# RWKV final states of the samples: made inside the chunk chain, their two products tied behind the entry's, and the spread tokens on VectorE instead of GpSimd

## The chip, the cores and the metric

One core of one Trainium2 chip runs the whole program in one launch. The metric is the device time of that core in microseconds (us); three runs of the kernel before gave 986.63, 986.88 and 988.02, median 986.88. A core has engines that each work through a queue of their own in order: TensorE (PE, with its weight loads PEld), VectorE (DVE), ScalarE (ACT), GpSimd (POOL) and SyncE (SP), which only issues DMAs here. They wait for each other through semaphores.

## The reference

One layer of a hybrid decoder: RWKV-7 time mixing and differential attention side by side, gates, an MLP, for 512 prompt tokens and 8 samples of 8 tokens each. The change touches RWKV's state for the samples:

```python
def step(S, inp):
    r_t, w_t, k_t, v_t, a_t, b_t = inp
    sa = jnp.einsum('bhij,bhj->bhi', S, a_t)
    S = S * w_t[:, :, None, :] + sa[..., None] * b_t[:, :, None, :] + v_t[..., None] * k_t[:, :, None, :]
    return S, jnp.einsum('bhij,bhj->bhi', S, r_t)

S, ys = lax.scan(step, S0.astype(jnp.float32), xs)
```

There are 8 heads of width 64, and the state `S` of each of the 8 samples after its 8 tokens is an output (`rwkv_sample`, here `Ss`), as is the prompt's (`Sp`).

## The kernel before

The scan is done in chunks of 64 tokens. Chunks 0 to 7 are the prompt; chunk 8 holds the 64 sample tokens, sample by sample. Heads go in pairs: head pair `hp` (0 to 3) fills 128 partitions, `par` 0 and 1 are its two heads. Two head pairs (`e` 0 and 1) share a chain: `chain(0)` runs pairs 0 and 1, `chain(1)` pairs 2 and 3.

`rwkv(hp)` is a generator in stages, parted by `yield`; `run(...)` takes the next stage of each pair that it names. The first stage makes decays, keys and the masked products `pA` (tiles `pn`, `pw`, `pa`, `pbn`, `KB`, `ST`, `pA`, `ABR`); then come the turned values `SVU`, the turned keys `KBt`, and the inverse `TT`. The stage that the change cuts is the one after `TT` (from L943): it spreads the solved tokens of chunk 8 over the samples, `vm = SVU[:, 8, par]` times a mask (128x512, one for each `par`), multiplies with `KBt` (product `pF`, two matmuls, each with 64 columns of weights and so into one half of `pF`'s partitions), adds the entering state `s0`, scales by the decay `pc`, and stores `Ss`.

A step of the chain for chunk `ci` (L1044 on): the entry (16 passes, `pch<-SVU,ST`), the copy `R` on VectorE, the solve (`pch<-R,TT`), the leaves of the chunk before (`pch<-SVU,ABR`), the copy of the solved `SVU` by VectorE and ScalarE together, the product with `KBt`, the new state `S<-S,pc,pch`, and `SVU<-S,pc` on both engines for the next entry. Chunk 8 is solved beside chunk 1, so its `SVU` is there from chunk 2 on.

TensorE's time between these steps is filled with dense products (`ps_z`, `ps_g`, `ps_brb`: 288 columns of tokens each). They stand in `waiting`; `take(n)` issues n of them at a low priority, and a scheduler that sorts each engine's instructions by priority, once their inputs are there by its own estimate, lays the final order. `tc.issue_after(x)` ties an instruction to a place behind `x`. `bank` gives one of three PSUM buffers (tag `w`), `tile(tag="G", bufs=3)` one of three SBUF buffers, which `vm` shares with other tiles; `s0` has two.

## Time and profile before

| | |
|---|---|
| median of three runs | 986.88 us |
| the profiled execution | 984.4 us, span 982.6 us |
| granted TensorE clock | 0.996 |
| chain 0 | about 284 to 327 us |
| chain 1 | about 432 to 475 us |
| `pF` products | 288.6 to 294.0 us and 482.8 to 486.9 us |
| `vm` on GpSimd, 8 of them | 1033 to 1043 ns each, 287.5 to 485.8 us |

The page gives busy time and share of the span by engine. The timeline gives start, length, engine, line, operation, tiles and count of instructions; what stands in brackets is the idle time of that engine ahead of it, and what ended it. A matmul's length covers its way through the array, so matmuls overlap: what one costs is read from the starts. An f32 matmul is recorded as two passes.

### The profile page before, as it was taken

The page shows a single profiled execution, that of the slowest core. Times are in us where ns is not written, and L with a number is a line of the kernel's source. Part 1 is how long each engine was busy: PE and PEld are TensorE (multiplying, and loading weights), DVE is VectorE, ACT ScalarE, POOL GpSimd, SP SyncE. Part 2 cuts the span into 40 slices and gives each one's busy share as a digit, 9 for nine tenths or more (in the row PEclk, how much of TensorE's full clock was granted, in tenths as well). Part 3 has the DMA queues.
Part 4 walks back from the last instruction along what each step waited for, and adds up shares of the span by engine and source line. Part 5 has one row for each costly group of instructions (what it writes and reads, how often), then busy time and mean ns, then how long its engine had stood idle before and what let it go on. Part 6 is the DMA issues. An engine that isn't in the chain of part 4 may idle for free.

```text
span 982.6 us, 24623 instructions
## 1 busy us (share of the span) xinstructions
PE 951.1 (97%) x10120; PEld 898.2 (91%) x10120; DVE 676.1 (69%) x1427; ACT 507.2 (52%) x1120; POOL 72.8 (7%) x181
## 2 busy tenths in 40 slices
PE   8999999999999998999999999999999999999996
PEld 8999989887978997878899999999999999999996
DVE  6698566875556848354787989966666666666744
ACT  6576455565345464543354767444444444444732
POOL 2611100100010210001300000000000000000001
PEclk9999999999999999999999999999999999999998
DMA  7422663201212225221477532222222232220402
GB/s 267 141 71 72 207 222 118 86 26 45 67 57 77 94 88 190 70 83 58 173 239 234 179 121 86 87 86 87 86 87 87 90 93 93 92 86 23 140 1 97
DMA packets 50833, 105.75 MB, mean 108 GB/s; under 512 B 6066, under 2 KB 8114, under 8 KB 50594
## 3 DMA queue, kind: packets, MB, share of 16 engines
q1 hardware_dynamic: 47442, 96.95, 30.6%
q0 software_dynamic: 1648, 5.35, 1.6%
q10 hardware_dynamic: 1632, 1.89, 0.6%
q8 instruction: 79, 1.29, 0.5%
q14 instruction: 32, 0.26, 0.1%
HBM read 89.38 MB, written 14.78 MB: 106 GB/s over the span
## 4 chain that ended last, share of the span: by engine, by line
PE 56%; DVE 2%; ACT 1%; DMA 1%; issue 1%; POOL 0%; DVEq 0%
PE ps_dn L72 20%; PE ua L1261 5%; PE ux L1261 5%; PE ps_wo L72 4%; PE ps_g L72 4%; PE ps_brb L72 3%; PE ps_bra L72 3%; PE uc L1261 3%; PE ub L1261 3%; PE ud L1261 2%; PE pch L1021 2%; DMA raw_dn<-in_w_down_dram 1%; PE pW L72 1%; PE pZ L72 0%; DVE ya L61 0%
## 5 line engine op out<-in xcount | busy, mean ns | idle before, releaser
L72 PE MATMUL ps_dn<-q,hi_dn 128*128 128x288 f32 x768 | 154.7, 296 | 0.0
L72 PEld LDWEIGHTS ps_dn<-q,hi_dn 128*128 128x128 f32 x768 | 122.8, 188 | 1.5
L72 PE MATMUL ps_dn<-q,lo_dn 128*128 128x288 f32 x384 | 113.2, 295 | 0.0
L72 PE MATMUL ps_g<-xh,hi_g 128*128 128x288 f32 x256 | 77.7, 303 | 1.0 <-DVE gg L61 1.0
L72 PE MATMUL ps_g<-xh,lo_g 128*128 128x288 f32 x256 | 78.5, 307 | 0.0
L72 PE MATMUL ps_g<-xl,hi_g 128*128 128x288 f32 x256 | 78.2, 305 | 0.0
L72 PEld LDWEIGHTS ps_dn<-q,lo_dn 128*128 128x128 f32 x384 | 72.0, 188 | 0.0
L72 PE MATMUL ps_z<-xh,lo_z 128*128 128x288 f32 (+1 forms) x224 | 69.7, 311 | 0.0
L72 PE MATMUL ps_z<-xl,hi_z 128*128 128x288 f32 (+1 forms) x224 | 67.2, 300 | 0.0
L72 PE MATMUL ps_z<-xh,hi_z 128*128 128x288 f32 (+1 forms) x224 | 67.1, 299 | 0.0
L61 DVE TENSOR_TENSOR ya<-ya,ps_dn 128x288 f32<-128x288 f32 x96 | 43.3, 451 | 27.6 <-PE ps_dn L72 27.5
L58 ACT ACTIVATE hi_dn<-raw_dn 128x512 fp32r<-128x512 f32 x48 | 30.1, 628 | 56.2 <-PE ps_dn L72 56.1
L58 ACT ACTIVATE c<-c 128x288 f32<-128x288 f32 x112 | 48.7, 439 | 9.4 <-DVE c L61 7.7
L1261 PE MATMUL ux<-h_t,hi 128*128 128x288 f32 x256 | 52.4, 297 | 0.0
L1261 PE MATMUL ua<-h_b,hi 128*128 128x288 f32 x256 | 52.2, 296 | 0.0
L72 PEld LDWEIGHTS ps_g<-xh,hi_g 128*128 128x128 f32 x256 | 48.2, 188 | 2.5 <-issue 1.4
L72 PEld LDWEIGHTS ps_g<-xl,hi_g 128*128 128x128 f32 x256 | 48.2, 188 | 1.8 <-issue 0.5
L58 ACT ACTIVATE hi<-a 128x1024 fp32r<-128x1024 f32 (+1 forms) x32 | 27.1, 846 | 43.3 <-PE ps_dn L72 34.9
L72 PEld LDWEIGHTS ps_g<-xh,lo_g 128*128 128x128 f32 x256 | 48.1, 188 | 1.4
L72 PE MATMUL ps_dn<-q,w 128*128 128x320 f32 (+1 forms) x336 | 46.6, 298 | 0.8 <-DVE fin L61 0.8
L72 PEld LDWEIGHTS ps_dn<-q,w 128*128 128x128 f32 x336 | 45.3, 190 | 1.2 <-DVE fin L61 1.1
L61 DVE TENSOR_TENSOR lo<-s,hi 128x1024 fp32r<-128x1024 f32 x32 | 39.2, 1224 | 10.4 <-ACT hi L58 10.3
(390 smaller groups left out, 2730.6 us busy)
## 6 DMA issues: line engine op xcount, KB each, us to landing
a<-in_w_up_dram SPq DMA_DIRECT2D x32, 512.0 KB, 3.3
raw_dn<-in_w_down_dram SPq DMA_DIRECT2D x64, 256.0 KB, 2.8
raw_g<-in_w_in_dram SPq DMA_DIRECT2D x32, 256.0 KB, 3.1
raw_z<-in_w_in_dram SPq DMA_DIRECT2D x28, 256.0 KB, 2.9
gt_d<-gg SPq DMA_DIRECT2D x16, 288.0 KB, 2.8
g<-gt_d SPq DMA_DIRECT2D x16, 288.0 KB, 3.7
kp<-in_ktab_dram SPq DMA_DIRECT2D x16, 256.0 KB, 3.5
vp<-in_vtab_dram SPq DMA_DIRECT2D x16, 256.0 KB, 3.5
```

What stands on the lines that cost most here:

```text
L58: ring["act"] = AE.activation(out=out, in_=in_, func=func, **kw)
L61: ins = (eng or VE).tensor_tensor(out=out, in0=a, in1=b, op=op)
L72: ring["mm"] = PE.matmul(out=out, lhsT=lhsT, rhs=rhs, start=start, stop=stop)
L1021: ring["mm"] = PE.matmul(out=ps[rows, e], lhsT=lhs, rhs=rhs, start=first and e == 1, stop=True, skip_group_check=True)
L1261: ring["mm"] = PE.matmul(out=ps[:, :288], lhsT=l[:, k], rhs=hb[blk][:, h, k], start=start and i == 0, stop=i == 11, skip_group_check=skip)
```

## The change

The stage after `TT` is cut in two by a new `yield`: first the two `vm`, now on VectorE (`GE` is gone from the call), then the two products and the rest. The two products are tied, the first behind the last matmul issued before, the second behind the first. `chain` now runs these two stages itself, right after the entry of a chunk: in chunk 2 the first pair's `vm`, in chunk 4 the first pair's products and the second pair's `vm`, in chunk 6 the second pair's products. So the matmul that the first product is tied to is the entry's last. The calls of `run` around the chains lose the stages that the chains took over.

```diff
@@ -940,15 +940,19 @@
         own[e] = ST, KBt, TT, ABR, pc
         yield
 
-        pF = bank(f"pF{hp}")
         vms = []
         for par in range(2):
             vm = rt.tile([P, NB, 64], F32, tag="G", bufs=3, name=f"vm{hp}{par}")
             tt(vm, m3(SVU[:, 8, par], NB),
-               c[:, C_MB:C_MB + NB].rearrange("p (b o) -> p b o", o=1).broadcast_to([P, NB, 64]), MUL, GE)
+               c[:, C_MB:C_MB + NB].rearrange("p (b o) -> p b o", o=1).broadcast_to([P, NB, 64]), MUL)
             vms.append(vm)
+        yield
+
+        pF = bank(f"pF{hp}")
+        lead = ring["mm"]
         for par, rows in halves:
-            mm(pF[rows], KBt[:, 8, par], vms[par].rearrange("p b i -> p (b i)"))
+            with tc.issue_after(lead.ins):
+                lead = mm(pF[rows], KBt[:, 8, par], vms[par].rearrange("p b i -> p (b i)"))
         sn = s0
         tt(sn, s0, pF.rearrange("p (b i) -> p b i", b=NB), ADD)
@@ -1041,9 +1045,12 @@
         owed = []
+        states = {2: (0,), 4: (0, 1), 6: (1,)}
         for ci in range(8):
             here = [(cbank(ci % 2, f"pch{pr}{ci}"), ci)]
             R = entry(*here[0])
+            for hp in states.get(ci, ()):
+                next(gens[2 * pr + hp])
             if ci == 1:
@@ -1098,7 +1105,7 @@
     chain(0)
-    run(0, 1, 2)
+    run(2)
     take(310)
@@ -1109,7 +1116,7 @@
     chain(1)
     take(226)
-    run(2, 3, 2, 3)
+    run(2, 3)
```

Where this moves instructions, first TensorE in chain 0. Before, the first product `pF0` stands ahead of the entry of chunk 2; behind that entry follow (`pch02<-R02` is the solve, `ABR` the leaves, `pn2` the beginning of head pair 2's first stage):

```order
L72 MATMUL pF0_4768<-vm01_4771,KBt0_2885 64x512
L72 MATMUL pF1_4778<-vm10_4779,KBt1_3722 64x512
L1021 MATMUL pch02_4558<-R02_4567,TT1_4432 64x64 x2
L1021 MATMUL pch02_4558<-R02_4567,TT0_3527 64x64 x2
L1021 MATMUL pch01_4508<-SVU0_2871,ABR1_3657 64x64 x2
L1021 MATMUL pch01_4508<-SVU0_2871,ABR0_2819 64x64 x2
L1021 MATMUL pch08_4519<-SVU0_2871,ABR1_3657 64x64 x2
L1021 MATMUL pch08_4519<-SVU0_2871,ABR0_2819 64x64 x2
L72 MATMUL pF1_4778<-vm11_4781,KBt1_3722 64x512
L72 MATMUL pn2_4790<-cst_sb_75,sq_2_4788 128x2 x5
```

Now the two `pF0` stand between entry and solve of chunk 4, the two `pF1` between those of chunk 6:

```order
L1025 MATMUL pch06_4709<-SVU0_2871,ST0_0_2814 64x64
L72 MATMUL pF1_4720<-vm10_4650,KBt1_3722 64x512
L72 MATMUL pF1_4720<-vm11_4652,KBt1_3722 64x512
L1025 MATMUL pch06_4709<-R06_4718,TT1_4432 64x64 x2
L1025 MATMUL pch06_4709<-R06_4718,TT0_3527 64x64 x2
L1025 MATMUL pch05_4676<-SVU0_2871,ABR1_3657 64x64 x2
L1025 MATMUL pch05_4676<-SVU0_2871,ABR0_2819 64x64 x2
L72 MATMUL pn2_4790<-cst_sb_75,sq_2_4788 128x2 x5
L72 MATMUL pw20_4818<-P12_1817,wl_215 128x288
L72 MATMUL pa20_4821<-P12_1817,al_216 128x288
L1025 MATMUL pch06_4709<-SVU0_2871,KBt1_3722 64x64 x2
```

So the products of one head pair stand together, and head pair 2's first stage begins in chunk 6 instead of chunk 2. Before, its products `pA2` stood at the end of chain 0, among chunk 7's product with `KBt` and its leaves; now 83 matmuls of fill lie between `pn2` and `pA2`, and `pA2` comes after the chain.

VectorE in chain 0 around chunk 2 (`SVU0<-pch01` and `<-pch08` are the solved chunks 1 and 8, `S01` the state after chunk 1, `R02` the copy behind the entry of chunk 2). Before:

```order
L1036 COPY SVU0_2871<-pch08_4519 64x2x64
L66 SCALAR_TENSOR_TENSOR S01_4551<-S00_4502,pc0_2791,pch01_4508 128x64
L66 SCALAR_TENSOR_TENSOR S01_4551<-S00_4502,pc1_3629,pch01_4508 128x64
L69 TENSOR_SCALAR SVU0_2871<-S01_4551,pc0_2791 64x64
L69 TENSOR_SCALAR SVU0_2871<-S01_4551,pc1_3629 64x64
L1029 COPY R02_4567<-pch02_4558 128x128
L61 TENSOR_TENSOR s0_0_2907<-s0_0_2907,pF0_4768 128x512
```

Now:

```order
L1040 COPY SVU0_2871<-pch08_4519 64x2x64
L61 TENSOR_TENSOR vm00_4569<-SVU0_2871,cst_sb_75 128x512
L66 SCALAR_TENSOR_TENSOR S01_4551<-S00_4502,pc0_2791,pch01_4508 128x64
L66 SCALAR_TENSOR_TENSOR S01_4551<-S00_4502,pc1_3629,pch01_4508 128x64
L69 TENSOR_SCALAR SVU0_2871<-S01_4551,pc0_2791 64x64
L69 TENSOR_SCALAR SVU0_2871<-S01_4551,pc1_3629 64x64
L61 TENSOR_TENSOR vm01_4571<-SVU0_2871,cst_sb_75 128x512
L61 TENSOR_TENSOR vm10_4650<-SVU0_2871,cst_sb_75 128x512
L1033 COPY R02_4567<-pch02_4558 128x128
```

Three of the four `vm` stand around that step; the fourth, `vm11`, comes behind `R04`, followed by the addition `s0<-s0,pF0` and then the copy `SVU0<-pch04`.

TensorE in chain 1. Before, the four products stand far behind the chain, among the dense products `ps_brb`:

```order
L72 MATMUL ps_brb_3_0_7427<-obh4_7094,lo_brb_3_0_7424 128x288
L72 MATMUL pF2_7438<-vm20_7439,KBt2_5393 64x512
L72 MATMUL pF2_7438<-vm21_7441,KBt2_5393 64x512
L72 MATMUL pF3_7448<-vm30_7449,KBt3_6226 64x512
L72 MATMUL pF3_7448<-vm31_7451,KBt3_6226 64x512
L72 MATMUL ps_brb_3_0_7427<-obh6_7100,hi_brb_3_0_7423 128x288
```

Now, in chunk 4 (and with `pF3` in chunk 6):

```order
L1025 MATMUL pch14_6945<-SVU2_5371,ST0_2_4866 64x64
L72 MATMUL pF2_6956<-vm20_6881,KBt2_5393 64x512
L72 MATMUL pF2_6956<-vm21_6883,KBt2_5393 64x512
L1025 MATMUL pch14_6945<-R14_6954,TT3_6696 64x64 x2
L1025 MATMUL pch14_6945<-R14_6954,TT2_6137 64x64 x2
L1025 MATMUL pch13_6912<-SVU2_5371,ABR3_5533 64x64 x2
```

The fills that stood between entry and solve of those chunks stand behind the leaves now, and the entries of chunks 5 and 6, which had fill between their first matmul and the other seven, stand whole. On GpSimd, `vm31` stood behind two powers `var`; none of the eight `vm` is left there. In SP's queue the loads of `s0` for pairs 2 and 3 stand two and four weight loads later.

## The prediction

> **What bounds the kernel now.** I read the page first, then the waits, then the timeline around the two stretches that hold the products `pF`.

> ```profile
> span 982.6 us, 24623 instructions
> PE 951.1 (97%) x10120; PEld 898.2 (91%) x10120; DVE 676.1 (69%) x1427; ACT 507.2 (52%) x1120; POOL 72.8 (7%) x181
> ```

> The reader is to see that TensorE (PE) is busy 97% of the span, VectorE (DVE) only 69%, ScalarE 52% and GpSimd (POOL) 7%. The dense work ("fill": the `ps_` matmuls) is put between the steps of the chain, so a microsecond counts only if PE stands still in it, or if PE does the same work in fewer slots. PE idles 982.6 - 951.1 = 31.5 us in all: no removal of waits can bring more than that. The same number of matmuls is issued after the change, so I look for idle time at `pF`, for products that run beside each other, and for changes between fill and chain matmuls.

> Chain 0, the timeline of PE (start, length, engine, line, tile):

> ```profile
> 288.63 1.07 PE L72 MATMUL pF<-vm,KBt 128*64 128x512 f32 x2
> 289.27 0.33 PE L1021 MATMUL pch<-SVU,ST 128*64 128x64 f32 x2
> 290.69 0.62 PE L1021 MATMUL pch<-SVU,ST 128*64 128x64 f32 x13 [0.98 <-DVE SVU L69]
> ...
> 291.20 1.02 PE L72 MATMUL pF<-vm,KBt 128*64 128x512 f32 x3
> 292.16 0.45 PE L1021 MATMUL pch<-R,TT 64*64 64x64 f32 x8
> ...
> 293.00 1.07 PE L72 MATMUL pF<-vm,KBt 128*64 128x512 f32 x2
> 294.00 1.28 PE L72 MATMUL pn<-cst_sb,sq 128*128 128x2 f32 x10
> ```

> One f32 product is two passes, so `x2` is one product. In chain 0 the first and the last of the four run alone for about 1 us each; only the middle two share the array. Within them the entry of chunk 2 stops after two passes and PE waits 0.98 us for VectorE's `SVU<-S`. The next view says why that is late:

> ```profile
> 287.54 4.05 POOL L61 TENSOR_TENSOR vm<-SVU,cst_sb 128x512 f32<-128x512 f32 x4 [30.84 <-DMA gt_d<-gg]
> ...
> 288.71 1.92 DVE L69 TENSOR_SCALAR SVU<-S,pc 64x64 f32<-64x64 f32 x2
> ...
> 319.47 0.40 DVE L69 TENSOR_SCALAR SVU<-S,pc 64x64 f32<-64x64 f32 x2
> ...
> 442.00 3.05 POOL L61 TENSOR_TENSOR vm<-SVU,cst_sb 128x512 f32<-128x512 f32 x3 [4.18 <-DVE SVU L1036]
> 442.65 1.44 DVE L69 TENSOR_SCALAR SVU<-S,pc 64x64 f32<-64x64 f32 x2
> 444.15 0.68 PE L1021 MATMUL pch<-SVU,ST 128*64 128x64 f32 x14 [0.50 <-DVE SVU L69]
> ```

> The same two `SVU<-S` instructions take 0.40 us where GpSimd is quiet, and 1.92 and 1.44 us while it makes `vm`. They end at 290.63 and 444.09; whole `vm` instructions of about 1.02 us end near 290.6 (the third) and 444.05 (the second). So VectorE is held until a `vm` is done. In both chains PE then waits, 0.98 and 0.50 us.

> The products of chain 1 come much later, behind the chain:

> ```profile
> 482.58 0.29 PE L72 MATMUL ps_brb<-obh,lo_brb 128*128 128x288 f32 x1
> 482.81 1.93 PE L72 MATMUL pF<-vm,KBt 128*64 128x512 f32 x6
> 485.87 1.07 PE L72 MATMUL pF<-vm,KBt 128*64 128x512 f32 x2 [1.13 <-POOL vm L61]
> 486.87 0.54 PE L72 MATMUL ps_brb<-obh,hi_brb 128*128 128x288 f32 x2
> ```

> The fourth `vm` is late (in GpSimd's order two powers of `var` stand ahead of it), and PE waits 1.13 us for it. Three products in 1.93 us, and one alone in 1.0 (485.87 to 486.87): a pair that is ready takes about 0.95 us, hardly more than one.

> **The change part by part.** The four edits have one answer on PE, so I work them out by stretch. First the price of an edge between fill and chain work, which each regrouping pays:

> ```profile
> 463.99 0.29 PE L72 MATMUL ps_g<-xh,lo_g 128*128 128x288 f32 x1
> 464.21 0.33 PE L1021 MATMUL pch<-SVU,ST 128*64 128x64 f32 x2
> 464.47 0.40 PE L72 MATMUL ps_g<-xh,hi_g 128*128 128x288 f32 x1
> 464.70 0.30 PE L72 MATMUL ps_g<-xl,hi_g 128*128 128x288 f32 x1
> 464.84 0.29 PE L72 MATMUL ps_g<-xh,lo_g 128*128 128x288 f32 x1
> 465.06 0.68 PE L1021 MATMUL pch<-SVU,ST 128*64 128x64 f32 x14
> 465.67 0.40 PE L72 MATMUL ps_g<-xh,hi_g 128*128 128x288 f32 x1
> 465.91 0.30 PE L72 MATMUL ps_g<-xl,hi_g 128*128 128x288 f32 x1
> ```

> This is one entry of 16 passes, cut in two by three fills. Fill follows fill in 0.13 to 0.14 us (464.70 to 464.84). Going in costs 465.06 - 464.84 - 0.13 = 0.09, coming out 465.91 - 465.67 - 0.13 = 0.11: 0.2 us per group of chain matmuls. The 14 passes alone cost 1.07 - 2 x 0.13 = 0.81, so a whole entry, two passes of 0.04 more, about 0.85. The cut one costs 463.99 to 465.91 less its five fill slots, 1.92 - 0.66 = 1.26: a cut is 0.4 us dearer.

> Chain 0, removed: from 288.63 less the edge (288.54) to 294.00 are 5.5 us. There remain the entry (0.85) and the solve with two leaves (292.16 to 293.00, 0.84, and one pair of edges, 0.2): 1.89. So **-3.6 us**, with the 0.98 of waiting in it.

> Added: two pairs, each tied right behind an entry in chunks 4 and 6 and followed by the solve. I take 1.05 us a pair, between 1.0 for one alone and 1.07 for the middle two with their run-out (the row of 291.20 is their second half; the solve begins at 292.16). The fills that stood between entry and solve go elsewhere, which saves one pair of edges, 0.2: 2 x 0.85 = **+1.7 us**.

> Moved: the last products of chain 0 and the first stage of the third head pair (`pn2` to `pA2`) no longer share groups; by the order of PE two groups more at the end: **+0.4 us**.

> Chain 1: the stretch 482.71 to 486.87 goes, with its edges 4.2 us (1.13 waiting in it); two pairs come, +1.7; the wait of 0.50 at 444.15 goes; and two entries that were cut in two (chunks 5 and 6) stand whole: 2 x 0.4 = 0.8. Sum -4.2 + 1.7 - 0.5 - 0.8 = **-3.8 us**.

> On VectorE: eight `vm`. No row shows one there; the nearest on the same engine is

> ```profile
> L61 DVE TENSOR_TENSOR s<-a 128x512 f32<-128x512 f32 x16 | 10.9, 684 | 0.0
> ```

> and above it lies GpSimd's own pace (3.05 us for three). I take 0.68, same shape and engine: 5.5 us of VectorE in all, 8.1 at the upper end. On the path it costs 0 if all lie in gaps and 5.5 (8.1) if none does; a gain below zero is left out, as the waits that GpSimd caused are counted above. I take 0 because of where they stand: `vm00` falls before `S<-S` of chunk 1, in VectorE's gap after the copies of chunk 1; `vm01` and `vm10` lie under nine and seven fills (1.2 and 0.9 us). The tightest are `vm11` and `vm31`, which must wait for a first product to give its buffer back, with the addition `s<-s,pF` behind them and then the chain's own copy `SVU<-pch`. For that the latency of a plain step, from solve to copy:

> ```profile
> 317.12 0.45 PE L1021 MATMUL pch<-R,TT 64*64 64x64 f32 x8
> ...
> 317.62 0.28 DVE L1036 COPY SVU<-pch 64x128 f32<-64x128 f32 x1 [0.82 <-PE pch L1021]
> ```

> From the start of an entry: products done at about 1.6, `vm11` to 2.25, addition to 2.9, copy to 3.2, ScalarE's half of it, as long again, to 3.5 us. PE reaches the product with `KBt` after pair, solve, leave and eleven fills at 0.5 + 1.0 + 0.3 + 0.3 + 1.65 = 3.75. The margin is 0.2 us: free, but barely. Without that cover each of the two places costs what it is late.

> The stage `pn2` to `pA2` gets shorter. Its rows on PE, and the window over it (PE, PEld, DVE, ACT, POOL busy, then clock and DMA):

> ```profile
> 297.03 0.65 PE L72 MATMUL pw<-P,wl 128*128 128x288 f32 x2
> ...
> 325.22 0.43 PE L72 MATMUL pA<-ST,KB 64*64 64x128 f32 x2
> 294.00:326.00 32.00, 31.59 (x349) 26.24 (x348) 21.01 (x55) 17.01 (x42) 2.88 (x12) 1.00 0.26 86
> ```

> It was spread over 294.00 to 325.22, 31.2 us, with VectorE busy two thirds of the window (21.01 of 32). In the new order 83 fills (11.0 us), six groups of chain work (0.5 to 0.85 each, some 3.5) and the stage's own matmuls (`pn` 1.28, six like the `pw` above, whose 0.65 overlaps with the next, at 0.5) stand between: about 18.5 us. Of VectorE's 21 us some 16 fall into it, since three of the five chain steps of that window now run earlier (four operations of 0.28 to 0.47 us each, 1.6 a step). It fits, but closely, and PE would wait at `pbn` or `pA`. Bounds: 0, and 31.2 - 18.5 = 12.7 if it takes as long as before; I take **+0.5**, near the lower, because there VectorE followed the chain and was not full.

> SP's two loads of `s0` move behind weight loads, which are issued ahead of their use, so I cost it at nothing. GpSimd's stores of the states come earlier, or a few microseconds later; nobody waits.

> Sum: -3.6 + 1.7 + 0.4 - 3.8 + 0.5 = **-4.8 us**. The profiled execution took 984.4 us (span 982.6), so 979.6; the median of the runs shown is 986.88, 2.5 above it, and gives **982.1 us**.

> **Rivals.** (a) VectorE becomes what the chain waits for: no gap takes a `vm`, each delays a step by some 0.62 us that fill does not hide. Then 8 x 0.62 = 5.0 comes back: 987.1, no change. For it: margins of 0.2. Against it: VectorE idles a third of that stretch. [...]

> (b) The slower one: the shortened stage. VectorE's and ScalarE's work from `pn2` to `pA2` lasts longer than the 18.5 us of PE work laid over it, and PE, in order, waits at `pbn2` and `pA2`. It has eaten the gain when PE waits 5.3 us there, makes the kernel measurably slower from 7.3 us, and at the full 12.7 gives 982.1 - 0.5 + 12.7 = 994.3. For it: the 16 us of VectorE in 18.5. Against it: in the window VectorE stood idle a third of the time, waiting for the chain.

> (c) The change does not do what it says on one point: `SVU<-S` was not held by GpSimd but by its place in the chain. Then 0.98 + 0.50 stays: 983.6. Against it: both ends fall on the end of a `vm`.

> (d) The tied pairs don't run beside each other: four times 0.95 more, 985.9. Against it: six passes in 1.93 us.

> **How the numbers follow.** Forecast 0.60 (its own range 980 to 984), (a) 0.14, (b) 0.08, (c) 0.08, (d) 0.06, others 0.04. A measurement of this kernel can tell about 0.2%, 2 us, from no change. Faster by more than that: the forecast, (c) and part of the rest, 0.74; within: (a), (d) and some of (b), 0.18; slower 0.08. The range leaves out the lower half of the forecast's tail and most of (b) and reaches to (d) and nearly to (a): 979.3 to 986.6.

> **What would show it.** Right: no wait above 0.3 us at an entry for `SVU L69`; `SVU<-S` pairs at 0.40 us everywhere; four passes of a `pF` pair within 1.1 us, four times; no `pF` behind 480 us; no `vm` on POOL. Wrong: waits on PE at `pbn` or `pA` for VectorE over 1 us (b); waits at `KBt` products of chunk 4 for `SVU` (a); a pair in 2 us (d); a `SVU<-S` pair still over 1 us (c). A PE idle sum that falls by less than 2 us makes the prediction wrong.

## The result and the profile after

The changed kernel takes 977.75 us (median of 4 runs, 977.14 to 980.07) beside 986.75 before (median of 4): ratio 0.9915, interval 0.9892 to 0.9939. Run once more without an edit, beside 29 runs of before, it took 977.24 against 985.12: 0.9923, interval 0.9909 to 0.9938. The prediction said 982.1, with a range of 979.3 to 986.6: the direction was right, and the forecast gain of 4.8 us was about half of the 9.0 between these medians. The page of the changed kernel begins:

```profile
span 978.3 us, 24613 instructions
PE 948.2 (97%) x10120; PEld 898.2 (92%) x10120; DVE 677.1 (69%) x1435; ACT 508.5 (52%) x1120; POOL 64.8 (7%) x173
```

The two profiled spans differ by 4.3 us only (982.6 and 978.3), which is less than the medians say. The page can't tell why; the same fill matmuls, read in both traces, can. First before, then after: start, length, engine, line, tile, of four fills of the same count, ahead of chain 0, behind the stage that follows it, ahead of chain 1 and behind its products.

```profile
287.29 0.40 PE L72 MATMUL ps_g<-xh,lo_g 128*128 128x288 f32 x1
...
357.38 0.38 PE L72 MATMUL ps_g<-xh,hi_g 128*128 128x288 f32 x1
...
433.68 0.30 PE L72 MATMUL ps_brb<-obh,hi_brb 128*128 128x288 f32 x1
...
492.56 0.30 PE L72 MATMUL ps_brb<-obh,lo_brb 128*128 128x288 f32 x1
```

```profile
289.18 0.40 PE L72 MATMUL ps_g<-xh,lo_g 128*128 128x288 f32 x1
...
356.17 0.38 PE L72 MATMUL ps_g<-xh,hi_g 128*128 128x288 f32 x1
...
432.47 0.29 PE L72 MATMUL ps_brb<-obh,hi_brb 128*128 128x288 f32 x1
...
487.78 0.29 PE L72 MATMUL ps_brb<-obh,lo_brb 128*128 128x288 f32 x1
```

Between the first two, and between the last two, both kernels issue the same matmuls, only in another order. The changed kernel starts the first of these fills 1.89 us later, the second 1.21 earlier, the third 1.21 earlier and the fourth 4.78 earlier. So chain 0 with what follows gained **3.1 us**, chain 1 **3.6 us**, 6.7 together, and the 1.89 was lost before any changed instruction ran. Half of it is in this row of the windows (PE, PEld, DVE, ACT, POOL busy, then the granted clock), of after and of before:

```profile
6.00:12.00 6.00, 5.58 (x28) 5.36 (x29) 4.60 (x7) 5.46 (x10) 1.60 (x4) 0.72 1.01 364
```

```profile
6.00:12.00 6.00, 5.31 (x35) 4.85 (x36) 4.71 (x7) 5.38 (x10) 1.41 (x3) 1.00 1.01 363
```

In this one execution of the changed kernel the clock of TensorE stood at 0.72 of full in that window (28 matmuls for 35); the other profile of it does not show that, and gains the same in the two stretches: 3.1 and 3.6 us. The rest of the 1.89 lies in small steps between 215 and 285 us that I did not follow up.

Chain 0 on VectorE, in answer to the rows with 1.92 us:

```profile
289.38 0.69 DVE L61 TENSOR_TENSOR vm<-SVU,cst_sb 128x512 f32<-128x512 f32 x1
...
290.60 0.40 DVE L69 TENSOR_SCALAR SVU<-S,pc 64x64 f32<-64x64 f32 x2
290.92 1.28 DVE L61 TENSOR_TENSOR vm<-SVU,cst_sb 128x512 f32<-128x512 f32 x2
```

The pair of `SVU<-S` takes 0.40 us, and one `vm` 0.69 (0.68 was taken). On PE, chunk 6 of chain 0:

```profile
314.16 0.69 PE L1025 MATMUL pch<-SVU,ST 128*64 128x64 f32 x16
314.67 1.03 PE L72 MATMUL pF<-vm,KBt 128*64 128x512 f32 x4
315.63 0.45 PE L1025 MATMUL pch<-R,TT 64*64 64x64 f32 x8
```

Entry, pair, solve: the four passes of two products take 1.03 us (1.05 was taken), and so in three of the four places. In chunk 4 of chain 0 one pass of the entry stands between the first pass and the other three, and the four span 1.13 us.

**Where the 3.1 us of chain 0 come from.** A matmul's slot is the time from its start to the start of the next. The slots of the same matmuls between the first two fills above, summed by kind:

| kind | before, us | after, us | difference |
|---|---|---|---|
| entries `pch<-SVU,ST` (96) | 5.21 | 3.70 | -1.51 |
| products `pF` (8 passes) | 2.64 | 1.97 | -0.67 |
| `pA` (72) | 3.18 | 2.48 | -0.70 |
| `pbn` (4) | 0.85 | 0.54 | -0.31 |
| fills (301), with edges | 46.71 | 46.16 | -0.55 |
| `pK` (9) | 1.25 | 1.60 | +0.34 |
| `pch<-SVU,ABR` (64) | 2.37 | 2.59 | +0.22 |
| `pw` (4) | 1.06 | 1.16 | +0.10 |

The first two lines are what the prediction counted. `pA` and `pbn` belong to the stage that it expected to lose. The line of `pK` is a wait of 0.44 us for ScalarE that before did not have. Before, the passes of `pA` were mixed with the last steps of the chain:

```profile
325.22 0.43 PE L72 MATMUL pA<-ST,KB 64*64 64x128 f32 x2
325.58 0.45 PE L1021 MATMUL pch<-SVU,KBt 128*64 128x64 f32 x8
325.96 0.65 PE L72 MATMUL pA<-ST,KB 64*64 64x128 f32 x12
326.67 0.27 PE L1021 MATMUL pch<-SVU,ABR 64*64 64x64 f32 x2
326.70 0.32 PE L72 MATMUL pA<-ST,KB 64*64 64x128 f32 x1
...
328.88 1.29 PE L72 MATMUL pA<-ST,KB 64*64 64x128 f32 x32 [0.51 <-DVE ABR L61]
```

After, they stand together, and PE waits a little longer for the mask:

```profile
335.46 1.32 PE L72 MATMUL pA<-ST,KB 64*64 64x128 f32 x40
...
338.11 1.29 PE L72 MATMUL pA<-ST,KB 64*64 64x128 f32 x32 [0.73 <-DVE ABR L61]
```

The wait rose from 0.51 to 0.73, but 72 passes in two groups cost less than in six. The line of the fills hides a wait that is gone. Before, VectorE and then PE, behind the stage:

```profile
345.47 0.76 DVE L61 TENSOR_TENSOR y<-y,var 128x576 f32<-128x576 f32 x1 [1.91 <-POOL var L243]
346.15 0.45 DVE L61 TENSOR_TENSOR gg<-ps_g,R 128x288 f32<-128x288 f32 x1
...
346.75 0.37 PE L72 MATMUL ps_g<-xh,hi_g 128*128 128x288 f32 x1 [0.99 <-DVE gg L61]
```

VectorE stood 1.91 us for GpSimd's `var` with the drain of a fill's bank (`gg`) queued behind it, and PE stood 0.99. With the later stage VectorE has other work ahead of that point, and PE does not wait.

**Where the 3.6 us of chain 1 come from.** By the same count the products `pF` give 2.14, the entries 1.52, and the fills lose 0.08. In the fills stands a new wait, ahead of the last fill that the comparison uses:

```profile
484.09 0.50 PE L72 MATMUL ps_brb<-obh,hi_brb 128*128 128x288 f32 x2 [0.69 <-DVE gb L66]
```

It is a drain once more (`gb` empties a bank of `ps_brb`): VectorE came to it late, after 1.49 us of waiting for GpSimd's `var`.

### The profile page after: what moved, and what is told of

Read it like the earlier page. It is cut to its first block, busy times and chain, and to the rows that moved or that the text cites. A ratio compares the mean times of both kernels' runs of the same rounds, so it can differ in the third digit from the quotient of the medians.

```text
span 978.3 us, 24613 instructions
## 1 busy us (share of the span) xinstructions
PE 948.2 (97%) x10120; PEld 898.2 (92%) x10120; DVE 677.1 (69%) x1435; ACT 508.5 (52%) x1120; POOL 64.8 (7%) x173
## 3 DMA queue, kind: packets, MB, share of 16 engines
q10 hardware_dynamic: 1632, 1.89, 0.6%
## 4 chain that ended last, share of the span: by engine, by line
PE 54%; DVE 3%; ACT 1%; DMA 1%; issue 1%; POOL 0%; DVEq 0%; SPq 0%; ACTq 0%
PE ps_dn L72 20%; PE ua L1268 5%; PE ux L1268 5%; PE ps_wo L72 4%; PE ps_g L72 3%; PE uc L1268 3%; PE ub L1268 3%; PE ps_brb L72 3%; PE ud L1268 2%; PE ps_bra L72 2%; PE pch L1025 2%; DMA raw_dn<-in_w_down_dram 1%; PE pW L72 1%; PE pZ L72 0%; DMA xr<-in_xT_dram 0%
## 5 line engine op out<-in xcount | busy, mean ns | idle before, releaser
L72 PE MATMUL ps_dn<-q,hi_dn 128*128 128x288 f32 x768 | 154.7, 296 | 0.0
L72 PEld LDWEIGHTS ps_dn<-q,hi_dn 128*128 128x128 f32 x768 | 122.8, 188 | 1.5
L72 PE MATMUL ps_dn<-q,lo_dn 128*128 128x288 f32 x384 | 113.2, 295 | 0.0
L72 PE MATMUL ps_g<-xh,lo_g 128*128 128x288 f32 x256 | 78.7, 307 | 0.0
L72 PE MATMUL ps_g<-xl,hi_g 128*128 128x288 f32 x256 | 78.1, 305 | 0.0
L72 PE MATMUL ps_g<-xh,hi_g 128*128 128x288 f32 x256 | 77.5, 303 | 0.0
L72 PEld LDWEIGHTS ps_dn<-q,lo_dn 128*128 128x128 f32 x384 | 72.1, 188 | 0.0
L72 PE MATMUL ps_z<-xh,lo_z 128*128 128x288 f32 (+1 forms) x224 | 69.7, 311 | 0.0
L72 PE MATMUL ps_z<-xl,hi_z 128*128 128x288 f32 (+1 forms) x224 | 67.2, 300 | 0.0
L72 PE MATMUL ps_z<-xh,hi_z 128*128 128x288 f32 (+1 forms) x224 | 67.1, 300 | 0.0
L61 DVE TENSOR_TENSOR ya<-ya,ps_dn 128x288 f32<-128x288 f32 x96 | 43.3, 451 | 27.6 <-PE ps_dn L72 27.4
L72 PEld LDWEIGHTS ps_g<-xl,hi_g 128*128 128x128 f32 x256 | 48.2, 188 | 1.8 <-issue 0.5
L72 PEld LDWEIGHTS ps_g<-xh,lo_g 128*128 128x128 f32 x256 | 48.1, 188 | 1.5
L72 PEld LDWEIGHTS ps_g<-xh,hi_g 128*128 128x128 f32 x256 | 48.3, 189 | 1.2 <-issue 0.2
L72 PE MATMUL ps_dn<-q,w 128*128 128x320 f32 (+1 forms) x336 | 46.6, 298 | 1.4 <-DVE fin L61 1.4
L72 PEld LDWEIGHTS ps_dn<-q,w 128*128 128x128 f32 x336 | 45.3, 190 | 1.7 <-DVE fin L61 1.7
L61 DVE TENSOR_TENSOR lo<-s,hi 128x1024 fp32r<-128x1024 f32 x32 | 39.2, 1224 | 10.4 <-ACT hi L58 10.3
```

What stands on the lines that cost most here:

```text
L61: ins = (eng or VE).tensor_tensor(out=out, in0=a, in1=b, op=op)
L72: ring["mm"] = PE.matmul(out=out, lhsT=lhsT, rhs=rhs, start=start, stop=stop)
```

## The experiments

All comparisons below use the same reading: the two stretches between the fills above (chain 0 from 287.29 to 357.38 of before, chain 1 from 433.68 to 492.56), and the time of several runs beside runs of before on the same chip.

**The change again.**

> The changed kernel once more, five rounds, nothing edited. Theory 1 (the two chains are all): between equal matmuls of the two profiles the changed kernel gains 2.2 us in chain 0 (the start of a fill at 287.3 to one at 342.8), 0.9 behind it where a wait for `gg` is gone, and 3.6 in chain 1, 6.7 us in all; the rest of the 9.0 us between the medians is scatter of the executions of before (984.4 to 988.0). Then the ratio comes out at 0.993 (6 to 7.5 us less), and a second profile shows these three steps again within 0.3 us. Theory 2 (something that the profiled pair does not show, in the shared stretches outside the chains): 0.9915 or less again, and a profile in which stretches outside the chains are 2 us shorter too.

977.24 us, ratio 0.9923 (0.9909 to 0.9938), so 7.6 less by the ratio, just above theory 1's 6 to 7.5, which lies within the interval. Its profile gives 3.1 and 3.6 us in the two stretches again, and no stretch outside the chains is 2 us shorter. The 0.9915 of the first comparison is within the interval of the second; theory 1 holds better than theory 2, and the first four runs of before (984.68 to 988.02) lie high beside the 29 (983.2 to 987.1).

**The engine alone.**

```diff
-               c[...].broadcast_to([P, NB, 64]), MUL, GE)
+               c[...].broadcast_to([P, NB, 64]), MUL)
```

> Only the four spread products of a pair by VectorE in place of GpSimd; the stages stay behind the chains, as before. Theory 1 (the place gives most): `SVU<-S` falls to 0.40 us, so the waits of 0.98 and 0.50 on PE go, 1.5 us; the fourth `vm` of chain 1 stands behind the multiplications of `y` on VectorE, so the wait of about 1.1 us at the last `pF` stays; 1 to 2 us less than before (985.0 to 986.0 beside 986.8). [...]

986.14 us, ratio 1.0011 (1.0002 to 1.0021): no gain, a loss if anything. The waits of 0.98 and 0.50 are gone, as expected. Chain 0 keeps 0.6: its entries give 1.05, but all four products now run singly, which costs 0.43. Chain 1 loses 1.4, and most of that starts in the place of the old wait of 1.13 (VectorE and PE of this kernel's second profile):

```profile
485.26 0.76 DVE L61 TENSOR_TENSOR y<-y,var 128x576 f32<-128x576 f32 x1 [0.41 <-POOL var L243]
485.93 0.68 DVE L61 TENSOR_TENSOR s<-s,pF 128x512 f32<-128x512 f32 x1
486.53 0.69 DVE L61 TENSOR_TENSOR vm<-SVU,cst_sb 128x512 f32<-128x512 f32 x1
...
487.27 1.07 PE L72 MATMUL pF<-vm,KBt 128*64 128x512 f32 x2 [2.51 <-DVE vm L61]
```

The fourth `vm` must wait until a product frees a buffer, and on VectorE it stands behind work that waits for GpSimd: PE waits 2.51 us. The "about 1.1" was wrong; the wait more than doubled. The longer wait alone would only have used up what chain 1's entries gain (1.4 against 1.3). The rest is the clock: right behind the wait thirteen fills start 0.24 us apart, where fills take 0.13 elsewhere, which with the edges of that stretch is 1.5 us. The experiment on the clock below comes back to it.

**The place alone** (new stages and ties, `vm` by GpSimd).

```diff
-               c[...].broadcast_to([P, NB, 64]), MUL)
+               c[...].broadcast_to([P, NB, 64]), MUL, GE)
```

> The new places and the ties, but `vm` made by GpSimd as before. TensorE's order is the changed kernel's but for a few fills. Theory 1 (place gives most, the engine 1 to 2.5 us): two `SVU<-S` of chunk 2 take over 1 us in each chain again, and PE waits 0.5 to 1.0 us there, twice; `vm` by GpSimd is also late at chunk 4 or not; 4 to 6 us less than before (981 to 983). Rival (the engine gives most): within 2 us of before.

982.41 us, ratio 0.9972 (0.9961 to 0.9983), 2.7 less: inside the range of microseconds, below the gain expected. GpSimd and VectorE, then PE, in chain 0:

```profile
287.81 3.05 POOL L61 TENSOR_TENSOR vm<-SVU,cst_sb 128x512 f32<-128x512 f32 x3 [31.32 <-DMA gt_d<-gg]
288.98 1.93 DVE L69 TENSOR_SCALAR SVU<-S,pc 64x64 f32<-64x64 f32 x2
...
290.96 0.68 PE L1025 MATMUL pch<-SVU,ST 128*64 128x64 f32 x14 [0.98 <-DVE SVU L69]
```

The two `SVU<-S` take 1.93 us and end where the third `vm` ends; in chain 1 it is 1.44 us and a wait of 0.50. In the changed kernel, with the same places and `vm` on VectorE, the pair takes 0.40 us. So rival (c) of the prediction falls: it is GpSimd that holds them, not their place. A new wait of 0.98 us appears behind chain 1, again a drain (`gg`) queued on VectorE behind a wait for `var`. The stretches give 2.3 us in chain 0 and 1.3 in chain 1.

**The places without the ties.**

```diff
-            with tc.issue_after(lead.ins):
-                lead = mm(pF[rows], KBt[...], ...)
+            mm(pF[rows], KBt[...], ...)
```

> The changed kernel without the ties: the products are written at the same places but may stand anywhere. In chain 0 all four products then stand around chunk 2 again, singly, in the order that the engine-only kernel has; in chain 1 around chunk 2 as well, not behind the chain. Theory 1 (a pair in one slot and the shorter tail of chain 0 count): two to four products run alone at about 0.95 us each, and the stage `pn2` to `pA2` shares its groups with the chain as before; 2 to 4 us slower than the changed kernel, 3 to 5 less than before. Rival (the ties are worth nothing, all is the engine and chain 1's place): within 1 us of the changed kernel.

982.84 us, ratio 0.9978 (0.9968 to 0.9988): 5.6 us above the changed kernel, more than expected. Chain 0 gains 0.6, chain 1 1.4. PE in chain 0:

```profile
289.56 1.07 PE L72 MATMUL pF<-vm,KBt 128*64 128x512 f32 x2
...
290.76 0.59 PE L72 MATMUL pF<-vm,KBt 128*64 128x512 f32 x1
...
291.19 0.59 PE L72 MATMUL pF<-vm,KBt 128*64 128x512 f32 x1
...
292.44 1.07 PE L72 MATMUL pF<-vm,KBt 128*64 128x512 f32 x2
...
294.29 1.07 PE L72 MATMUL pF<-vm,KBt 128*64 128x512 f32 x2
295.29 1.28 PE L72 MATMUL pn<-cst_sb,sq 128*128 128x2 f32 x10
```

Written in chunks 4 and 6, the products run singly around chunk 2 all the same, and the next stage with them. The tie is what puts the products where the code has them.

**One chain at a time.**

For chain 0 alone (the kernel for chain 1 alone has `pr == 1`, and `run(0, 0, 1, 1, 2)` behind chain 0 in place of `run(2)`):

```diff
-        states = {2: (0,), 4: (0, 1), 6: (1,)}
+        states = {2: (0,), 4: (0, 1), 6: (1,)} if pr == 0 else {}
...
-    run(2, 3)
+    run(2, 2, 3, 3, 2, 3)
```

> The new places and ties in chain 0 alone; in chain 1 the two stages run one after the other behind the chain, with `vm` on VectorE. Theory 1 (the parts add up): chain 0 and the fills behind it give 3.1 us as in the changed kernel (2.2 to the fill at 342.8, 0.9 at `gg`), chain 1 gives nothing or loses up to 1.4, since there the fourth `vm` on VectorE was 2.51 us late in the engine-only kernel: 1.5 to 3.5 us less than before (981.6 to 983.6). Rival (the gain is in chain 1, chain 0 is worth the 1.0 that the prediction gave it): 1 us less or nothing.

> The new places and ties in chain 1 alone; behind chain 0 the two stages run as in before, with `vm` on VectorE, and TensorE's order has the four products at the chain's end, tied to each other. Theory 1: chain 1 gives 3.6 us as in the changed kernel; chain 0 loses its wait of 0.98 and a cut entry but keeps four products behind the chain with the stage `pn2` among them, 0 to 2 us; 3.5 to 5.5 us less than before (979.6 to 981.6). Rival (the chains depend on each other, through fills that both draw on): outside this range, or chain 1's stretch off 3.6 by more than 0.5.

Chain 0 alone: 982.43 us, 0.9974 (0.9963 to 0.9985); 3.1 us gained in chain 0, 1.4 lost in chain 1 with the same wait, now 2.52, and the same slow fills behind it. Chain 1 alone: 980.00 us, 0.9956 (0.9940 to 0.9972); 3.6 gained in chain 1 and 0.6 in chain 0. Each chain gives in its own stretch what it gives in the full change, to 0.05 us, and the other chain what the engine alone gave there: they don't depend on each other.

**The later stage alone.** This undoes no part of the change; it gives the kernel before the one side effect that the prediction had as a loss.

```diff
-            mm(pn[:, 2 * t:2 * t + 2], sq[:, o:o + P], c[:, C_HS:C_HS + 2])
+            with tc.issue_after(pair[0]["c6"].ins) if hp == 2 else nullcontext():
+                mm(pn[:, 2 * t:2 * t + 2], sq[:, o:o + P], c[:, C_HS:C_HS + 2])
...
+            if ci == 6:
+                own["c6"] = ring["mm"]
```

> The kernel before with one thing moved: the first matmuls of the stage `pn2` to `pA2` are tied behind chunk 6 of chain 0, as they come to stand in the changed kernel; `vm` by GpSimd, products untied at chunk 2. Theory 1 (the shorter stage gains, where the prediction had it cost 0.5): its `pA` passes stand in two groups, not six, 0.7 less; `pbn` 0.3 less; the wait of 0.99 for `gg` behind it goes; the wait of 0.98 for `SVU<-S` stays; 1.5 to 2.5 us less than before (982.6 to 983.6). Rival (the prediction's step: a shorter stage squeezes VectorE): no gain or up to 1 us slower, with a longer wait at `pA` (over 0.7) and at `pbn`.

The stretch of chain 0 gains 1.6 us, with the products untouched, as theory 1 said (rows of its second profile):

```profile
333.80 1.32 PE L72 MATMUL pA<-ST,KB 64*64 64x128 f32 x40
336.75 1.29 PE L72 MATMUL pA<-ST,KB 64*64 64x128 f32 x32 [0.65 <-DVE ABR L61]
```

`pA` costs 0.71 less, `pbn` 0.31 less, the wait for `gg` is gone, and the wait at the mask is 0.65. But the time, 984.19 us, is not told apart from before: 0.9997 (0.9989 to 1.0006). Right behind the stretch its first profile shows the clock at 0.72, and a second profile of the same kernel does not:

```profile
360.00:366.00 6.00, 6.00 (x28) 5.10 (x27) 1.58 (x3) 2.60 (x6) 1.87 (x10) 0.72 0.00 0
```

```profile
360.00:366.00 6.00, 6.00 (x40) 5.58 (x40) 3.00 (x6) 3.80 (x12) 1.88 (x10) 1.00 0.00 0
```

> The kernel with the late stage, profiled once more, nothing edited. Theory (phase): chain 0 to the fill at 357 gives 1.58 us again, with `pA` in two groups and no wait for `gg`; the halved clock near 360 us may be absent, and then the span is 981 to 981.5. Rival (the halved clock is what the late stage brings): it is there again at the same place.

> The kernel before, profiled once more. Theory (the halved clock of 3.5 us at 360 us comes with the phase of a window, not with the change): the waits of 0.98, 0.99, 0.50 and 1.13 us are there again within 0.1; a stretch of clock 0.50 may or may not stand behind the narrow products `pn` near 362 us. Rival (the clock falls there only where `vm` or the stage was moved): never in this kernel.

From the fill at 357 to one at 379, the first lost 1.64 us on before, the second 0.01. The 1.6 us of the stage are there in both profiles, and the second has a span of 980.6, a little under the 981 to 981.5 expected. But before, profiled again, has a span of 980.6 too, with all its waits (0.98, 0.98, 0.50, 1.13) and full clock there: stretches that the edit doesn't touch differ by as much. So the gain of the stage is shown in the trace and not in the time.

The granted clocks of the single runs tell most of why. Among the profiles, those in which the clock never drops ahead of the program's end have a mean granted clock of 0.996 or 0.997, those with one drop 0.994 or 0.995. By that measure 9 of the 12 runs of the late stage had at least one drop, and 6 of the 24 of before. The three without one took 983.5 us on average, beside 984.3 for the 18 of before; the nine with one took 984.6, beside 986.0 for the 6: like with like the late stage is 0.8 to 1.5 us faster. The groups are small, so this is a reading of the record and not a test. Why the drop comes more often was not shown; the last section has what the profiles tell of its place.

**A long wait and the clock.**

> The engine-only kernel, profiled once more, nothing edited. Theory (a long wait of TensorE halves its clock): the wait of 2.51 us for the fourth `vm` is there again, and within 2 us behind it a stretch of clock 0.50 of about 3.5 us. Rival (the halved clock comes at random): the wait is there, the clock stays 1.00.

The wait of 2.51 us is there again (the rows above are of this profile), and behind it:

```profile
486.00:492.00 6.00, 4.73 (x18) 3.92 (x19) 3.56 (x7) 0.04 (x1) 1.14 (x2) 0.72 0.56 203
```

All three profiles with this wait (both of the engine alone, and chain 0 alone) have the drop there, and none of the eleven others, where the longest wait at that place is 2.06 us. The theory holds for these. It makes no rule yet: in all three the drop also stands 37 steps of 3.4133 us behind the one near 362 us (see the last section), and no run has the wait elsewhere.

**Other chunks.**

```diff
-        states = {2: (0,), 4: (0, 1), 6: (1,)}
+        states = {2: (0,), 3: (0, 1), 5: (1,)}
```

> The changed kernel with the states one chunk earlier (chunks 2, 3 and 5 in place of 2, 4 and 6). TensorE's order loses the cut of the entry of chunk 4 in chain 0, 0.4 us; the stage `pn2` to `pA2` starts one chunk earlier, so `pA` stands closer to its operands' old distance and its wait of 0.73 may go; against it, the second `vm` of chunk 3 waits for a product and then stands ahead of the chain's own copy, with fewer fills over it. Theory 1 (the pairs are free wherever they are tied behind an entry): the same as the changed kernel to 1 us less (976.2 to 977.2). Rival (the place in the chain matters): 1 to 2 us slower than the changed kernel, with waits for `SVU` at chunk 3.

981.52 us, 0.9971 (0.9958 to 0.9985). In its profile chain 0 gains 4.0 rather than 3.1, but chain 1 only 2.4, with a wait of 0.99 for `gb` in it, and 1.65 is lost right behind it (VectorE, then PE):

```profile
486.91 0.76 DVE L61 TENSOR_TENSOR y<-y,var 128x576 f32<-128x576 f32 x1 [1.91 <-POOL var L243]
487.58 0.81 DVE L66 SCALAR_TENSOR_TENSOR gb<-gb,ps_brb 128x288 f32<-128x288 f32 x2
...
488.18 0.50 PE L72 MATMUL ps_brb<-obh,hi_brb 128*128 128x288 f32 x2 [2.06 <-DVE gb L66]
```

The rival named the wrong instruction (`SVU` at chunk 3 is not waited for over 0.4 us) but was right that place matters: VectorE's order changes, and a drain falls behind a wait for GpSimd once more. The profile is that of the fastest of the eight runs (977.82 us at a granted clock of 0.997); the others took 980.4 to 982.7 at 0.993 to 0.996, so the trace does not show what they lost, and whether the wait of 2.06 can bring the drop of the clock stays open. Taking the earlier chunks in chain 0 alone:

> Chunks 2, 3 and 5 in chain 0, chunks 2, 4 and 6 in chain 1: each chain at the places where its profile was better. Theory 1 (the chains add up): chain 0 and the fills behind it give 4.0 us as in the kernel with the earlier chunks (2.83 and 1.16), chain 1 gives 3.6 as in the changed kernel, 7.6 in all, so 0.5 to 1.3 us less than the changed kernel (976.0 to 976.8 beside 977.2), and the wait of 2.06 for `gb` behind chain 1, which the kernel with the earlier chunks had, is not there. Rival (what chain 0 gains comes back later as such a wait): the same as the changed kernel or slower.

976.88 us, 0.9925 (0.9911 to 0.9939) beside the changed kernel's 0.9923 in another comparison. The trace gives 4.0 and 3.6 us, 7.6 in all, and no such wait, as expected; in time it can't be told from the changed kernel.

## Why the prediction was wrong

- **Chain 0, products and entries** (-3.6 + 1.7 = -1.9): the lines of entries and `pF` sum to -1.51 - 0.67 = -2.18. Right, the waits at `SVU<-S` with it.
- **Chain 1** (-3.8): -3.6. The terms were right (`pF` and the entries, -2.14 and -1.52); the wait of 0.69 for `gb` was not foreseen.
- **The stage `pn2` to `pA2`** (+0.4 for more groups, +0.5 for the squeeze): this is the step that failed. The prediction read the window 294 to 326 for VectorE's room and asked only how long PE would have to wait. In the changed kernel the rest of the stretch, beside entries and `pF`, gave -0.9 instead of +0.9; in the late-stage kernel, where nothing else moves, the same move gave -1.6. (The +0.22 of `ABR` stands in that kernel too, so it belongs here.) The prediction did not count that `pA` and `pbn` stop sharing groups with the chain, 1.0 us by the table, nor that the wait of 0.99 for `gg` behind the window would go, a row that it never read. The squeeze exists, but is 0.2 us (0.51 to 0.73 at the mask).
- **The sum**: -1.9 - 3.8 + 0.9 = -4.8 was predicted; -2.2 - 3.6 - 0.9 = -6.7 was measured in the stretches. Of the 1.9 between them the failed step makes up 1.8; the other two are off by 0.3 and 0.2, in opposite directions.
- **The base**: the sum against the profiled execution gave 979.6. Carrying it to the median of three runs added 2.5 us. The 64 runs of before taken since have a median of 984.7, close to the 984.4 of the profiled one. With that base and -6.7 the forecast would have been 977.7 to 978.0. Of the miss of 4.35 us, somewhat more than half is the base.
- **Rivals**: (a) did not come in the changed kernel, where the waits on PE have no step of a chain that waits for VectorE over 0.2 us; in the engine-only kernel it did, at one place, where PE waits 2.51 us instead of 1.13. (b) fell: 0.73 us at `pA`, nothing over 0.25 at `pbn2`. (c) fell by the place-only kernel. (d) fell: 1.03 us a pair.
- **A test of its own that misled**: it called the prediction wrong if PE's idle sum fell by less than 2 us. It fell by 1.4 (31.5 to 30.1) while the stretches gained 6.7. Part of the gain is in busy time (951.1 to 948.2): products that ran alone, and groups with edges, count as busy.

The parts don't add up over engine and place: 1.0 us lost by the engine alone (its chain 1 has the slow fills, worth 1.5), 2.7 gained by the place alone, 7.6 by both. In chain 0 `vm` on VectorE gives 0.6 by itself; in chain 1 it pays only where the products leave the chain's end, and the places pay in full only when GpSimd stays off `SVU<-S`. Over the two chains they do add up: 3.1 and 3.6.

## What to carry to other kernels

Where a scheduler fills in, writing a product at a place does nothing; only a dependency holds it there, and what a moved product pulls along or lets go behind it can be worth as much as the product. When a stage moves, read the waits just behind its window and how many groups its matmuls stand in, not only whether its engine has room. Compare two kernels by the start of the same matmul in both traces before and after each changed stretch: here that repeated to 0.05 us where the spans of two executions of one kernel differed by 0.9 to 2.1 us. And ask whether the clock fell inside the stretch before a loss is put down to a wait: here one drop cost up to 1.67 us.

## What the runs showed of the hardware

The drops of one profile begin whole numbers of 3.4133 us apart, in the four profiles in which two of them were read in half-microsecond windows:

| profile | drops begin at, us | steps of 3.4133 us between |
|---|---|---|
| changed kernel, first | 7.57, 970.13 (program's end) | 282 |
| engine alone, first | 7.58, 362.57, 488.86 | 104, 37 |
| engine alone, second | 362.15, 488.45 | 37 |
| chain 0 alone | 359.81, 486.10 | 37 |

Near 362 us stand 32 narrow products `pI` and 10 `pn` (64x16 and 128x2 for each pass), and PE is busy throughout. In the 6 profiles with a drop there, it begins 2.25 to 3.44 us behind the first `pI`. In before and in the first profile of the changed kernel, which have none there, the steps counted back from the drop at the program's end (974.91 and 970.13 us) fall 1.9 and 1.7 us behind it. How the steps lie against the products, which the expectations call the phase, differs between executions of one kernel: the engine alone has 3.11 and 2.79. And one kernel can have the drop in one execution and not in the next: the late stage has it in its first profile, 2.85 us behind the first `pI`, and not in its second. That the place of the steps against these products decides is the author's reading. By it a change that moves the products, as the late stage does, could make the drop come more often; two profiles of the late stage do not show that.
